# Half of the gated layers' z and u columns as seven block products, with weight sums made by accumulating DMAs

## The chip, the cores and the metric

One core of a Trainium2 chip runs the whole program: eight cores are there, seven have no part in it. The metric is the device time of one execution in microseconds, the median over the runs. The profile comes from one execution of its own.

## The reference, cut to what matters

Four residual layers work on x, 256 tokens of 1024 channels; their mixers are A, B, C and A again. The change touches the two A layers alone:

```python
def mixer_a(h, w_in, v_gain, w_s, b_s, w_out):
    proj = h @ w_in
    u = proj[..., :A_WIDTH]
    v = rms_norm(proj[..., A_WIDTH:2 * A_WIDTH], v_gain)
    z = proj[..., 2 * A_WIDTH:]
    ...
    mixed = jnp.einsum('gij,bcjgd->bcigd', ws, v) + b_s.T[None, None, :, :, None]
    ...
    y = u * mixed * jax.nn.silu(z)
    return y @ w_out
```

h is the normed x, 256 x 1024, and A_WIDTH is 2048, so u, v and z have four blocks of 512 columns each. The output is wanted in float32.

## The kernel before, in words

**Arithmetic.** Each float32 product is made as three matmuls of rounded parts (`mm3`, line 75): high by high, high by low and low by high. ACT makes a high part with a copy (`hi_of`, line 81, rows L82), DVE the low part with a subtraction (`lo_of`, line 84, rows L85).

**Weights.** The host cuts all weights into 272 units of 128 partitions x 1024 floats, 512 KB each, in the order of their use. A unit holds two k-tiles of 512 columns. SyncE loads a unit into one of four raw buffers `wr` (line 131), and ACT and DVE split it into one of seven pairs of buffers `w..h` and `w..l` (lines 142 to 152). The matmuls of a projection take the units in order (`next_unit`, line 156). After each k-tile `step` (line 163) first lets waiting tasks go on and then splits units up to five ahead of the one in use. A raw buffer is free once its low part is made, and the next load is issued then (line 154).

**Stationary operand.** h^T stands in two tiles, hTh and hTl, its high and low parts, 8 k-tiles x 256 tokens each (lines 188 and 189). `norm_transpose` (line 216) fills them for each layer. A projection by tokens (`proj_tok`, line 253) has two accumulators in PSUM, one for each 128 tokens, and takes every unit for both: 2 k-tiles x 2 token halves x 3 parts, 12 matmuls of 128x512. A block of 512 columns is four units, 48 matmuls.

**A gated layer** (`layer_a`, line 350) makes the four blocks of v, then for n = 0 to 3 the blocks z_n and u_n. Silu of z goes into a tile `sz` (line 449). `mix_task` (line 401) makes the twelve token-mixing matmuls `mx` of the block. `y_task` (line 415) makes y = u * silu(z) * (mx + b) on DVE (lines 423 and 426), transposes it on PE (line 434) and splits it. `proj_out` (line 291) is the output product, `wo`.

**What sets the order.** There is one program order. Each engine takes its instructions in that order and starts one when what it needs is there. Tasks are generators that `tick` (line 101) advances: a task gives out a few instructions and says after how many ticks it goes on. So what stands behind what on an engine is decided by the ticks, and a waiting instruction holds up all that follows on its engine. GpSimd's queue (POOL) holds the small constant loads (lines 340 to 343 and 466 to 472), the powers in the norms, and little else.

Of the kernel before, what the change touches and what calls it, by code (L numbers as in the profile page):

```python
# [17 lines left out]
P = 128  # L18
# [24 lines left out]
LAST_LAG = 1  # L43
LAST_AHEAD = 3
WARM = 24


@with_exitstack
def hybrid_trunk_kernel(ctx, tc, x, wts, norm_gainT, a_v_gain, a_wsT, a_bsT, b_gl, b_gv, c_scaleT,
# [31 lines left out]
    def hi_of(hi, src):  # L81
        nc.scalar.activation(hi, src, AF.Copy)  # L82

    def lo_of(lo, src, hi):
        nc.vector.tensor_tensor(lo, src, hi.bitcast(F32), op=ALU.subtract)  # L85
# [37 lines left out]
    used = [0]  # L123
    loaded = [0]
    split = [0]

    def load_units(n):
        while loaded[0] < min(n, n_units):
            u = loaded[0]
            raw = wp.tile([P, 2, HALF], F32, tag="wr", name=f"wr{u}", bufs=RAW_BUFS)  # L130
            nc.sync.dma_start(raw, wts[u].rearrange("p (k n) -> p k n", n=HALF))
            raws.append(raw)
            loaded[0] += 1

    lowered = [0]

    def split_hi(n):

        while split[0] < min(n, n_units):
            u = split[0]  # L140
            load_units(u + 1)
            hi, lo = pair(wp, [P, 2, HALF], "w", f"w{u}", W_BUFS)
            hi_of(hi, raws[u])
            units.append((hi, lo))
            split[0] += 1

    def split_units(n):

        split_hi(n)
        while lowered[0] < min(n, n_units):  # L150
            u = lowered[0]
            lo_of(units[u][1], raws[u], units[u][0])
            lowered[0] += 1
            load_units(u + 1 + RAW_BUFS)

    def next_unit():

# [2 lines left out]
        split_units(u + 1)  # L160
        return units[u]

    def step(i, ahead=AHEAD):

        tick()
        if i % 2 == 0:
            split_hi(used[0] + ahead)
        else:
            split_units(used[0] + ahead)
# [24 lines left out]
    gT = cp.tile([P, DEPTH * KT + 16], F32, tag="gT", name="gT")[:, :DEPTH * KT].rearrange(  # L194
        "p (l k) -> p l k", k=KT)
    nc.scalar.dma_start(gT, norm_gainT)


# [17 lines left out]
    def norm_transpose(layer, t, xs):  # L216

        pts = []
        for n in range(2):
            pt = (trp if n else atp)(f"hp{layer}{t}{n}").rearrange("p (k c) -> p k c", c=P)  # L220
            for k in range(4):
                nc.tensor.transpose(pt[:, k], xs[:, n, k * P:(k + 1) * P], ident)  # L222
            pts.append(pt)
        sl = slice(t * P, (t + 1) * P)
        for k in range(KT):
# [18 lines left out]

    def h_t(k, t):
        sl = slice(t * P, (t + 1) * P)
        return hTh[:, k, sl], hTl[:, k, sl]

    def h_all(k):
        return hTh[:, k, :], hTl[:, k, :]  # L250


    def proj_tok(name, skew=None):

        o = [pp(f"{name}_{t}") for t in range(2)]
        if skew is not None:
            ws = [next_unit() for j in range(4)]
            for t in range(2):
                need(("h", skew, t))
                for k in range(KT):  # L260
                    w = ws[k // 2]
                    mm3(o[t], h_t(k, t), (w[0][:, k % 2], w[1][:, k % 2]), k == 0, k == KT - 1)
# [12 lines left out]
        return o  # L275
# [72 lines left out]
        return kc, wsT, bsT  # L348

    def layer_a(layer, consts, pl, mid):  # L350
        kc, wsT, bsT = consts

        def tmp(tag, name, bufs):
            return pl.tile([P, HALF], F32, tag=tag, name=name, bufs=bufs)
# [5 lines left out]
        def v_task(n, o):  # L360
            vh, vl = pair(pl, [P, 2, HALF], "v", f"v{layer}{n}", 5)
            v.append((vh, vl))
            vv = [tmp("vv", f"vv{layer}{n}{t}", 2) for t in range(2)]
            for t in range(2):
                nc.scalar.activation(junk, o[t], AF.Square, accum_out=vs[t][:, n:n + 1])  # L365
                nc.vector.tensor_tensor(vv[t], o[t], kc[:, n * HALF:(n + 1) * HALF], op=ALU.mult)  # L366
            yield 1
            for t in range(2):
                hi_of(vh[:, t], vv[t])
            yield 1  # L370
            for t in range(2):
# [24 lines left out]
            mid()  # L396
# [18 lines left out]
        def y_task(n, up, us):  # L415
# [23 lines left out]
                    yield 1  # L439
            done.add(("y", layer, n))  # L440

        for n in range(4):
            spawn(v_task(n, proj_tok(f"v{layer}{n}", skew=layer if n == 0 else None)))
        for n in range(4):
            zp = proj_tok(f"z{layer}{n}")
            us = []
            for t in range(2):
                sz = tmp("sz", f"sz{layer}{n}{t}", 4)
                nc.scalar.activation(sz, zp[t], AF.Silu)  # L449
                us.append(sz)  # L450
            spawn(mix_task(n), 4)
            spawn(y_task(n, proj_tok(f"u{layer}{n}"), us))
# [28 lines left out]
                                        cs[:, a, t:t + 1, :].to_broadcast([P, 2 * NG, ROPE]), op=ALU.mult)  # L481

    def layer_b(layer, consts, pl):
        gv, msk, rop = consts
        m0, m1 = msk[:, :NG * P], msk[:, NG * P:]
        yT = []
# [241 lines left out]


    def layer_c(layer, pl):  # L730
        csc = pl.tile([P, 32], F32, name="csc")[:, :16]
        nc.gpsimd.dma_start(csc, c_scaleT)
        rcn = pl.tile([P, 4, PAD], F32, name="rcn")
# [2 lines left out]
        def tmp(tag, name, bufs):  # L736
            return pl.tile([P, HALF], F32, tag=tag, name=name, bufs=bufs)
# [309 lines left out]
```

## Time and profile before

| | |
|---|---|
| median of 3 runs | 847.01 us (846.98 to 847.21) |
| the profiled execution's own time | 846.98 us |
| its span, first to last instruction | 845.3 us |
| granted TensorE clock | 0.999 |
| PE busy | 834.2 us, 4600 matmuls |
| DVE busy, ACT busy, POOL busy | 546.7, 488.6, 56.8 us |
| loads of weight units | 272 of 512 KB, median 4.2 us from issue to landing |
| read from HBM over the span | 147.72 MB |

PE is TensorE's matmul row and PEld its weight loads, which overlap the matmuls. The time from one matmul's start to the next is its cost on a busy PE; its own duration is longer, since matmuls are pipelined. A gap in a row stands in brackets with what ended it. "L82" is a line of the kernel before; the kernel after has its own numbers.

### The profile page before, as it was taken

To read this page: it belongs to the slowest core of one execution; us is meant where nothing else is said; L and a number is where in the kernel's file an instruction comes from. 1 tells how busy PE (TensorE), PEld (TensorE's weight loads), DVE (VectorE), ACT (ScalarE), POOL (GpSimd) and SP (SyncE) were. 2 spreads that over 40 slices of the span, in tenths; PEclk is the share of its full clock that TensorE was granted. 3 is DMA by queue.
4 is the path that set the end of the run, shared out by engine and by line. 5 is a ranking of instruction groups with operands and counts; after the bars stand their busy time and mean duration, and the time that the engine had idled before them with its cause. 6 is when DMAs were issued, how large, how long until landed. Compare 5 with 4: busy or idle time off the path is not lost.

```text
span 845.3 us, 12424 instructions
## 1 busy us (share of the span) xinstructions
PE 834.2 (99%) x4600; PEld 719.2 (85%) x4600; DVE 546.7 (65%) x932; ACT 488.6 (58%) x918; POOL 56.8 (7%) x79
## 2 busy tenths in 40 slices
PE   8999999999999999999999999999999999999998
PEld 6888888888988888888888889999988888888886
DVE  6866556546747667667667576798754786556551
ACT  7665444336768677678678567446543666434340
POOL 1301000001001021021021011000000000000000
PEclk9999999999999999999999999999999999999999
DMA  8756554562755345345345267547664476455541
GB/s 297 268 207 218 197 199 155 180 193 93 253 173 157 119 150 175 124 151 174 125 150 172 79 220 255 176 150 243 203 206 149 140 235 213 158 176 172 174 149 50
DMA packets 41500, 149.57 MB, mean 177 GB/s; under 512 B 4864, under 2 KB 4880, under 8 KB 41184
## 3 DMA queue, kind: packets, MB, share of 16 engines
q1 hardware_dynamic: 40320, 144.72, 51.9%
q0 software_dynamic: 976, 4.05, 1.5%
q8 instruction: 36, 0.59, 0.3%
q14 instruction: 24, 0.20, 0.1%
q10 hardware_dynamic: 144, 0.02, 0.0%
HBM read 147.72 MB, written 1.05 MB: 176 GB/s over the span
## 4 chain that ended last, share of the span: by engine, by line
PE 86%; ACT 7%; DVE 2%; issue 2%; POOL 2%; DMA 1%; SPq 0%; POOLq 0%; DVEq 0%
PE wo L77 6%; PE wo L78 6%; PE wo L79 6%; PE qk L79 4%; PE qk L77 4%; PE qk L78 4%; PE u L79 3%; PE z L79 3%; PE z L77 3%; PE u L77 3%; PE u L78 3%; PE z L78 3%; PE v L79 3%; PE v L77 3%; PE v L78 3%; ACT junk L500 2%
## 5 line engine op out<-in xcount | busy, mean ns | idle before, releaser
L505 POOL TENSOR_TENSOR qr<-qm,m 128x4 f32<-128x4 f32 x24 | 30.3, 1271 | 224.4 <-DVE qm L504 224.4
L509 ACT ACTIVATE qn<-qk,qr 128x128 f32<-128x128 f32 x96 | 27.5, 381 | 15.1 <-POOL qr L505 15.1
L500 ACT ACTIVATE junk<-qk 128x128 bf16<-128x128 f32 x96 | 26.8, 279 | 7.3 <-PE qk L79 4.6
L423 DVE TENSOR_TENSOR sz<-u,sz 128x512 f32<-128x512 f32 x16 | 11.0, 686 | 28.0 <-PE u L79 28.0
L226 ACT ACTIVATE hTh<-hp,gT 128x128 fp32r<-128x128 f32 x64 | 17.5, 382 | 16.1 <-PE hp L222 16.1
L207 POOL TENSOR_TENSOR r<-ms,m 128x1 f32<-128x1 f32 x8 | 5.4, 670 | 285.7 <-DVE ms L205 285.7
L321 DVE TENSOR_TENSOR x<-wo,x 128x512 f32<-128x512 f32 x16 | 11.0, 690 | 20.1 <-PE wo L79 20.0
L229 DVE SCALAR_TENSOR_TENSOR hTl<-hp,gT,hTh 128x128 fp32r<-128x128 f32 x64 | 17.9, 343 | 7.8 <-ACT hTh L226 7.8
L365 ACT ACTIVATE junk<-v 128x512 bf16<-128x512 f32 x16 | 9.6, 600 | 18.1 <-PE v L79 17.9
L500 ACT ACTIVATION_READ_ACCUMULATOR junk<-qk 128x1 f32 x96 | 19.1, 199 | 0.0
L366 DVE TENSOR_TENSOR vv<-v,kc 128x512 f32<-128x512 f32 x16 | 10.9, 689 | 12.7 <-ACT junk L365 12.6
L449 ACT ACTIVATE sz<-z 128x512 f32<-128x512 f32 x16 | 9.4, 597 | 15.5 <-PE z L79 14.9
L518 DVE TENSOR_TENSOR ra<-qn,kcb 128x64 f32<-128x64 f32 x48 | 10.6, 221 | 12.0 <-ACT qn L509 10.9
L530 PE MATMUL qt<-ident,qn 128*128 128x128 f32 x96 | 14.6, 274 | 3.4 <-DVE qk12l L538 0.5
L530 PEld LDWEIGHTS qt<-ident,qn 128*128 128x128 f32 x96 | 11.3, 140 | 7.3 <-issue 2.7
L200 ACT ACTIVATE junk<-x 128x512 bf16<-128x512 f32 x16 | 10.2, 639 | 10.9 <-DVE x L321 9.4
L426 DVE SCALAR_TENSOR_TENSOR yy<-mx,bs,sz 128x256 f32<-128x256 f32 x32 | 14.0, 480 | 0.6
L600 ACT ACTIVATE p<-p,rl 128x384 f32<-128x384 f32 (+1 forms) x16 | 11.5, 769 | 4.8 <-DVE rl L599 4.8
L522 DVE TENSOR_TENSOR rb<-qn,kcb 128x32 f32<-128x32 f32 x96 | 13.8, 184 | 0.0
L596 ACT ACTIVATE p<-p,nb 128x768 f32<-128x768 f32 x8 | 7.5, 938 | 7.9 <-DVE nb L595 7.9
L504 DVE TENSOR_SCALAR qm<-qs 128x4 f32<-128x4 f32 x24 | 3.3, 165 | 12.7 <-ACT junk L500 12.7
L346 POOL TENSOR_SCALAR_AFFINE_SELECT kc<-kc 128x128 f32<-128x128 f32 x16 | 9.2, 612 | 15.4 <-DMA kc<-in_a_wsT_dram 15.4
(2770 smaller groups left out, 3262.0 us busy)
## 6 DMA issues: line engine op xcount, KB each, us to landing
wr<-in_wts_dram SPq DMA_DIRECT2D x272, 512.0 KB, 4.2
kc<-in_a_v_gain_dram POOLq DMA_DIRECT2D x2, 1024.0 KB, 6.1
x<-in_x_dram SPq DMA_DIRECT2D x4, 256.0 KB, 4.9
kc<-in_a_wsT_dram POOLq DMA_DIRECT2D x2, 512.0 KB, 8.8
out_dram<-x SPq DMA_DIRECT2D x4, 256.0 KB, 2.0
kcb<-in_masks_dram POOLq DMA_DIRECT2D x1, 576.0 KB, 8.5
kcb<-in_b_gl_dram POOLq DMA_DIRECT2D x1, 192.0 KB, 6.0
kcb<-in_rope_dram POOLq DMA_DIRECT2D x1, 64.0 KB, 8.4
```

The source lines that it names most:

```text
L77: nc.tensor.matmul(out_ap, lh[0], rh[0], start=start, stop=False, skip_group_check=True)
L78: nc.tensor.matmul(out_ap, lh[0], rh[1], start=False, stop=False, skip_group_check=True)
L79: nc.tensor.matmul(out_ap, lh[1], rh[0], start=False, stop=stop, skip_group_check=True)
L226: nc.scalar.activation(hTh[:, k, sl], pts[k // 4][:, k % 4], AF.Copy, scale=gT[:, layer, k:k + 1])
L229: nc.vector.scalar_tensor_tensor(hTl[:, k, sl], pts[k // 4][:, k % 4], gT[:, layer, k:k + 1], hTh[:, k, sl].bitcast(F32), op0=ALU.mult, op ...
L426: nc.vector.scalar_tensor_tensor(y[:, sl], mxs[n][t][:, sl], bsT[:, 2 * n + gg:2 * n + gg + 1], us[t][:, sl], op0=ALU.add, op1=ALU.mult)
L500: nc.scalar.activation(junk[:, :HD], ov[t][:, h], AF.Square, accum_out=ssq[t][:, h:h + 1])
L505: nc.gpsimd.tensor_tensor(rq[t], ms, m05, op=ALU.pow)
L509: nc.scalar.activation(qn[t][:, h], ov[t][:, h], AF.Copy, scale=rq[t][:, h:h + 1])
L522: nc.vector.tensor_tensor(rb[:, hs, s0:s0 + 16], qn[t][:, hs, s1:s1 + 16], c, op=ALU.mult)
L530: nc.tensor.transpose(pts[t][:, h], qn[t][:, h], ident)
L600: nc.scalar.activation(f, f, AF.Copy, scale=rl[i][:, 0:1])
```

## The change

In each A layer the blocks n = 1 and n = 3 of z and u are made together. Write h as a 2 x 2 matrix of blocks (two halves of 128 tokens, two halves of 512 channels) and the weights of z_n and u_n, side by side, as another: rows are the two channel halves, columns are z and u. The product of two such matrices takes eight block products, two in each of the four results. The change makes it with seven, in a known scheme of sums and differences (Winograd's form of Strassen's). Each product has four k-tiles, two units and one accumulator:

- the sums of h are made once per layer, by `sums_task` on DVE and ACT, in the v phase: four tiles, split into `sm..h` and `sm..l`
- the sums of weights are made while loading. A plain DMA brings one unit and a DMA of GpSimd adds another to the tile in place (`accum_op=ALU.add`). The list `seq` has 14 entries for a pair, in place of 8 units: the first two are u + z at k, kept in two tiles `ws`; two of z; two of u; then u is added to `ws` again; two of z; two of u + u in the `wr` buffers; then z is added to `ws`
- a product is made in one of four PSUM tiles, zb, xb, yb, wb; zb takes two products and xb three. ACT copies a partial result out (q5, p1), or its negative (n2, n3), before the next product is added to the same bank
- `first_task` and `second_task` form z and u from these on DVE, with Silu on ACT, and `mix_task` and `y_task` follow as before
- h^T becomes one tile with 16 floats to spare; in the layers A it starts 16 floats (64 bytes) higher, in B and C where it stood. gT loses the 16 floats it had to spare

The core of the diff:

```diff
+SEVEN = (1, 3)
...
+    def seven(z, u):
+        return [((u, z), "new"), ((z,), None), ((u + 2,), None), ((u + 2,), "on"), ((z + 2,), None),
+                ((u + 2, u), None), ((z + 2,), "on")]
...
+    def load_units(n=0, ahead=False):
+        while loaded[0] < n_seq and (loaded[0] < n or ahead and room()):
+            i = loaded[0]
+            us, sums = seq[i]
+            if sums and sums[:-1] == "on":
+                raw = summed[sums[-1]]
+            else:
...
+                nc.sync.dma_start(raw, wts[us[0]].rearrange("p (k n) -> p k n", n=HALF))
+                us = us[1:]
+            for u in us:
+                nc.gpsimd.dma_start(raw, wts[u].rearrange("p (k n) -> p k n", n=HALF), accum_op=ALU.add)
...
-    hTh = cp.tile([P, KT, S], F32R, tag="hTh", name="hTh")
-    hTl = cp.tile([P, KT, S], F32R, tag="hTl", name="hTl")
+    hT = cp.tile([P, 2 * KT * S + 16], F32R, tag="hT", name="hT")
+    def h_parts(layer):
+        o = 16 if layer in (0, DEPTH - 1) else 0
+        return [hT[:, o + i * KT * S:o + (i + 1) * KT * S].rearrange("p (k s) -> p k s", s=S) for i in range(2)]
...
+            zb = pp(f"zb{layer}{n}")
+            product(zb, sm(S_A21_A22), True)
+            spawn(keep_task("q5", keep, zb), 1)
+            xb = pp(f"xb{layer}{n}")
+            product(xb, lambda k: h_t(k, 0), True)
+            spawn(keep_task("p1", keep, xb), 1)
+            product(zb, sm(S_A12_REST), False)
+            product(xb, sm(S_REST), False)
+            spawn(keep_task("n2", minus, xb), 1)
+            yb = pp(f"yb{layer}{n}")
+            product(yb, lambda k: h_t(4 + k, 0), True)
...
+            spawn(first_task(), 1)
+            spawn(mix_task(n), 2)
+            product(xb, sm(S_A11_A21), False)
+            spawn(keep_task("n3", minus, xb), 1)
+            wb = pp(f"wb{layer}{n}")
+            product(wb, lambda k: h_t(4 + k, 1), True)
...
         for n in range(4):
+            if n in SEVEN:
+                seven_products(n)
+                continue
             zp = proj_tok(f"z{layer}{n}")
```

The units of the first pair are 24 to 31 before, and 24 to 37 after. GpSimd's queue before, between the second layer's constants and that layer's norm:

```order
L466 DMA kcb_661<-in_b_gl_dram 128x384
L468 DMA kcb_661<-in_masks_dram 128x1152
L470 DMA kcb_661<-in_rope_dram 128x128
L472 DMA gv_665<-in_b_gv_dram 128x6
L207 TENSOR_TENSOR r10_1633<-ms10_1631,m05_83 128x1
```

And now, at the same place; each row on `in_wts_dram` adds a unit to the tile it names:

```order
L611 DMA kcb_688<-in_b_gl_dram 128x384
L613 DMA kcb_688<-in_masks_dram 128x1152
L615 DMA kcb_688<-in_rope_dram 128x128
L617 DMA gv_692<-in_b_gv_dram 128x6
L175 DMA ws24_570<-in_wts_dram 128x1024
L175 DMA ws25_573<-in_wts_dram 128x1024
L175 DMA wr34_794<-in_wts_dram 128x1024
L175 DMA wr35_818<-in_wts_dram 128x1024
L175 DMA ws24_570<-in_wts_dram 128x1024
L175 DMA ws25_573<-in_wts_dram 128x1024
```

The additions for entries 30 and 31, 34 and 35, 36 and 37 stand behind the second layer's constants, in this order. The ones of 34 and 35 wait for the plain loads of the same tiles, and those of 36 and 37 stand behind them.

ACT before, in the pair z1,u1, from the high part of unit 34 on:

```order
L82 ACTIVATE w34h_903<-wr34_830 128x1024
L82 ACTIVATE w35h_935<-wr35_849 128x1024
L82 ACTIVATE w36h_953<-wr36_867 128x1024
L82 ACTIVATE w37h_983<-wr37_891 128x1024
L82 ACTIVATE y01h_965<-yp010_992 128x4x128
```

ACT now, from the copy p1 on:

```order
L537 ACTIVATE p101_881<-xb01_838 128x512
L83 ACTIVATE w34h_889<-wr34_794 128x1024
L83 ACTIVATE w35h_901<-wr35_818 128x1024
L83 ACTIVATE w36h_913<-ws24_570 128x1024
L83 ACTIVATE w37h_924<-ws25_573 128x1024
L532 ACTIVATE n201_930<-xb01_838 128x512
L83 ACTIVATE w38h_936<-wr38_869 128x1024
```

The copy n2 of xb, new on ACT, stands behind the high parts of entries 36 and 37, which read the tiles that GpSimd's last two additions of the pair fill.

DVE now, around the start of the pair; the rows on u, sz, mx and yy are `y_task` of block 0, and stood there before too:

```order
L86 TENSOR_TENSOR w28l_785<-wr28_657,w28h_784 128x1024
L474 TENSOR_TENSOR sz000_705<-u00_0_709,sz000_705 128x512
L477 SCALAR_TENSOR_TENSOR yy000_799<-mx000_743,bs0_187,sz000_705 128x256 x2
L474 TENSOR_TENSOR sz001_707<-u00_1_710,sz001_707 128x512
L477 SCALAR_TENSOR_TENSOR yy001_803<-mx001_750,bs0_187,sz001_707 128x256 x2
L86 TENSOR_TENSOR w29l_812<-wr29_679,w29h_811 128x1024
L86 TENSOR_TENSOR w30l_825<-ws24_570,w30h_824 128x1024
```

The low part of entry 29, behind which the load of entry 35 is issued, stands behind that gating, as unit 29's did.

More of the change, by code (lines that the diff above doesn't have):

```diff
@@ L224, in norm_transpose @@
         sl = slice(t * P, (t + 1) * P)
+        hTh, hTl = h_parts(layer)
         for k in range(KT):
@@ L440, in y_task, with sums_task @@
             done.add(("y", layer, n))
+        smh, sml = pair(pl, [P, 4, 4, P], "sm", f"sm{layer}", 1)
+        def sums_task():
+            q = {}
+            for k, t in ((1, 1), (0, 1), (0, 0), (1, 0)):
+                d = q[k, t] = tmp("sz", f"sq{layer}{k}{t}", 4).rearrange("p (k c) -> p k c", c=P)
+                hh, hl = (a[:, 4 * k:4 * k + 4, t * P:(t + 1) * P].bitcast(F32) for a in hcur)
+                nc.vector.tensor_tensor(d, hh, hl, op=ALU.add)
+                yield 1
+            a11, a12, a21, a22 = q[0, 0], q[1, 0], q[0, 1], q[1, 1]
+            for i, (d, a, b, op) in enumerate(((a22, a21, a22, ALU.subtract), (a21, a11, a21, ALU.subtract),
+                                               (a11, a22, a11, ALU.subtract), (a12, a12, a11, ALU.add))):
+                nc.vector.tensor_tensor(d, a, b, op=op)
+                hi_of(smh[:, i], d)
+                yield 1
+                lo_of(sml[:, i], d, smh[:, i])
+                yield 1
+            done.add(("sums", layer))
@@ new lines, in layer_a, with seven_products, sm, product @@
+        S_A21_A22, S_A11_A21, S_REST, S_A12_REST = range(4)
+        def seven_products(n):
+            need(("sums", layer))
+            def sm(i):
+                return lambda k: (smh[:, i, k], sml[:, i, k])
+            def product(o, a, first):
+                for j in range(2):
+                    w = next_unit()
+                    for kk in range(2):
+                        k = 2 * j + kk
+                        mm3(o, a(k), (w[0][:, kk], w[1][:, kk]), first and k == 0, k == 3)
+                        step(kk, due=kk == 1)
+            def minus(o, name):
+                d = tmp("vv", name, 2)
+                nc.scalar.activation(d, o, AF.Copy, scale=-1.0)
+                return d
+            def keep(o, name):
+                d = tmp("sz", name, 4)
+                nc.scalar.activation(d, o, AF.Copy)
+                return d
+            r = {}
+            def keep_task(key, how, o):
+                r[key] = how(o, f"{key}{layer}{n}")
+                yield 1
+            zb = pp(f"zb{layer}{n}")
[9 more added lines that the diff above has]
+            product(yb, lambda k: h_t(4 + k, 0), True)
+            z0, u0 = r["p1"], r["n2"]
+            def first_task():
+                nc.vector.tensor_tensor(z0, yb, z0, op=ALU.add)
+                nc.scalar.activation(z0, z0, AF.Silu)
+                yield 1
+                nc.vector.tensor_tensor(u0, zb, u0, op=ALU.add)
+            spawn(first_task(), 1)
[4 more added lines that the diff above has]
+            product(wb, lambda k: h_t(4 + k, 1), True)
+            z1, u1 = r["n3"], r["q5"]
+            def second_task():
+                nc.vector.tensor_tensor(u1, u1, z1, op=ALU.add)
+                nc.vector.tensor_tensor(z1, wb, z1, op=ALU.subtract)
+                nc.scalar.activation(z1, z1, AF.Silu)
+                yield 1
+            spawn(second_task(), 1)
+            spawn(y_task(n, (u0, u1), (z0, z1)), 2)
```

56 lines of the change are left out of this document (41 added, 15 removed).

## The prediction

> **What bounds the kernel now.** I read the page first: who is busy, and the chain that ended last.
>
> ```profile
> PE 834.2 (99%) x4600; PEld 719.2 (85%) x4600; DVE 546.7 (65%) x932; ACT 488.6 (58%) x918; POOL 56.8 (7%) x79
> PE 86%; ACT 7%; DVE 2%; issue 2%; POOL 2%; DMA 1%; SPq 0%; POOLq 0%; DVEq 0%
> ```
>
> PE is the bound, and the chain is 86% PE. So a matmul that disappears is worth its spacing on PE, as long as nothing new makes PE wait. Then I asked for the windows of the first gated layer, up to and through the columns z1,u1, which the change rewrites first:
>
> ```profile
> 34.00:51.00 17.00, 17.00 (x76) 13.95 (x75) 13.53 (x16) 12.74 (x21) 0.00 (x0) 1.00 0.67 233
> 56.00:67.00 11.00, 11.00 (x50) 9.03 (x49) 9.70 (x14) 9.58 (x13) 1.95 (x3) 1.00 0.45 154
> 67.00:79.60 12.60, 12.60 (x62) 10.58 (x61) 5.86 (x6) 6.26 (x8) 2.03 (x4) 1.00 0.83 269
> 79.60:103.70 24.10, 24.10 (x117) 20.09 (x116) 14.75 (x21) 10.31 (x12) 0.00 (x0) 1.00 0.59 195
> ```
>
> The columns are the stretch and then PE, PEld, DVE, ACT and POOL busy, the granted clock, the DMA share and GB/s. PE is busy in every microsecond of all four stretches, at clock 1.00. From 79.6 to 103.7 (the pair z1,u1) DVE works 14.75 of 24.1 us and ACT 10.31: there is room, but not for a doubling.
>
> **The change part by part.** The time is made against the profiled execution, 846.98 us with a span of 845.3; the median of the three runs is 847.01, so the two are the same. Below, a "unit" is one 512 KB weight tile, split by ACT into a high part and by DVE into a low part.
>
> *Fewer matmuls.* The spacing of 128x512 matmuls comes from starts in PE's timeline, 48 matmuls apart: first z0, then a stretch of wo.
>
> ```profile
> 56.20 0.39 PE L77 MATMUL z<-w16h,hTh 128*128 128x512 f32 x1
> 67.19 0.39 PE L77 MATMUL u<-w20h,hTh 128*128 128x512 f32 x1
> 805.65 0.39 PE L77 MATMUL wo<-w259h,y30h 128*128 128x512 f32 x1
> 816.53 0.39 PE L77 MATMUL wo<-w263h,y31h 128*128 128x512 f32 x1
> ```
>
> z takes (67.19 - 56.20)/48 = 0.2290 us a matmul, wo (816.53 - 805.65)/48 = 0.2267. A pair z,u has 96 matmuls now and 84 afterwards (7 products of 4 k-tiles and 3 parts). Four pairs lose 48: 48 x 0.2290 = **-11.0 us**.
>
> *h^T 64 bytes higher.* z and wo differ in the stationary operand. hTh begins, after tiles of 128-byte multiples and the 1088 bytes of junk, 64 bytes past a multiple of 128; y begins on a multiple. After the change h^T of the gated layers does too, and so do the new sums. If that is what makes wo faster, the 768 matmuls left in v, z and u and the 336 of the products gain 0.0023 us each: 1104 x 0.0023 = **-2.5 us**. It may also be nothing (0 is the other end, for the two differ in buffers as well). I take the full 2.5, as the wo rows are the only ones with such an operand at this shape.
>
> *Sums of h.* Twelve DVE operations of 128x512 in the v phase, about 0.69 us each (the rows below), are 8.3 us. In the three windows above from 34 to 51 and 56 to 79.6 DVE stands idle 3.5 + 1.3 + 6.7 = 11.5 us, and a unit is split some five units ahead of its use. I cost it at nothing. If that cover were gone, 34 to 51 alone would be short by 8.3 - 3.5 = 4.8 us per layer.
>
> *Splits.* A pair uses 14 units in place of 8, each for half as long. DVE's timeline at the start of z1, and PE's first row there:
>
> ```profile
> 70.32 1.22 DVE L85 TENSOR_TENSOR w26l<-wr,w26h 128x1024 fp32r<-128x1024 f32 x1
> 71.46 1.22 DVE L85 TENSOR_TENSOR w27l<-wr,w27h 128x1024 fp32r<-128x1024 f32 x1
> 79.12 0.69 DVE L423 TENSOR_TENSOR sz<-u,sz 128x512 f32<-128x512 f32 x1 [0.59 <-PE u L79]
> 79.84 0.88 DVE L426 SCALAR_TENSOR_TENSOR yy<-mx,bs,sz 128x256 f32<-128x256 f32 x2
> 82.14 1.22 DVE L85 TENSOR_TENSOR w29l<-wr,w29h 128x1024 fp32r<-128x1024 f32 x1
> 83.61 0.69 DVE L85 TENSOR_TENSOR y00l<-yp,y00h 128x512 fp32r<-128x512 f32 x1 [0.26 <-ACT y00h L82]
> 79.60 0.39 PE L77 MATMUL z<-w24h,hTh 128*128 128x512 f32 x1
> 82.35 0.60 PE L434 MATMUL yp<-ident,yy 128*128 128x128 f32 x4
> 82.70 0.47 PE L77 MATMUL z<-w25h,hTh 128*128 128x512 f32 x1
> ```
>
> A low part starts 1.14 us after the one ahead of it, the gating of y takes 82.14 - 79.12 = 3.0, a copy or an add 0.7. DVE's work in a new pair is 14 x 1.14 + 4 x 0.72 + 3.0 + 2 x 0.69 = 23.2 us. PE's is 84 x 0.2267 = 19.0, plus the twelve mx (1.4) and eight transposes (2 x 0.35): 21.2. DVE is over by 2.0 us, and the lead of five units (5 x 6 x 0.2267 = 6.8 us) covers that, since an ordinary pair or wo follows. I cost it at nothing; without the lead it costs 2.0 us a pair.
>
> *The sums of weights: a new wait.* This is the term that decides. The last two weight sums of a pair are made in place, on the tile that was split six units before, and Pool's queue holds them behind two other accumulates, the second of which waits for a plain load. On ACT the copy n2 (the product of units 7 and 8 with its sign turned) stands behind the high parts of both sums. The eleventh unit writes over the bank that n2 reads. So PE waits there for: plain load, accumulate, accumulate, accumulate, high part, copy. The prices of DMAs, each from the DMA issues of a window of one or two issues:
>
> ```profile
> wr<-in_wts_dram SPq DMA_DIRECT2D x1, 512.0 KB, 3.1
> wr<-in_wts_dram SPq DMA_DIRECT2D x1, 512.0 KB, 4.8
> wr<-in_wts_dram SPq DMA_DIRECT2D x1, 512.0 KB, 5.0
> kc<-in_a_v_gain_dram POOLq DMA_DIRECT2D x1, 1024.0 KB, 5.2
> kc<-in_a_wsT_dram POOLq DMA_DIRECT2D x1, 512.0 KB, 7.2
> ```
>
> The issues behind the first three, in SyncE's rows for wr, and two high parts and a copy in ACT's timeline:
>
> ```profile
> L131 SPq DMA_DIRECT2D wr<-in_wts_dram x1: 328/328/328, 83.4 to 83.4; - x1
> L131 SPq DMA_DIRECT2D wr<-in_wts_dram x1: 328/328/328, 41.3 to 41.3; - x1
> L131 SPq DMA_DIRECT2D wr<-in_wts_dram x1: 328/328/328, 43.6 to 43.6; - x1
> 68.09 1.06 ACT L82 ACTIVATE w25h<-wr 128x1024 fp32r<-128x1024 f32 x1
> 69.04 1.06 ACT L82 ACTIVATE w26h<-wr 128x1024 fp32r<-128x1024 f32 x1
> 82.98 0.60 ACT L82 ACTIVATE y00h<-yp 128x512 fp32r<-128x512 f32 x1 [4.37 <-PE yp L434]
> ```
>
> A lone 512 KB load lands 3.1 us after its issue. The loads issued at 41.3 and 43.6, with one between them, land at 46.1 and 48.6: 1.25 us of transfer each once they queue. The 1 MB load of Pool took 5.2, which is 2.7 plus two transfers.
>
> With T as the start of a pair (79.60): the low part that frees the buffer ends at 83.36, T + 3.8, and its load is issued there, landing at T + 6.9. Pool's overhead of 2.7 and three transfers of 1.25 put the last sum at T + 13.4. A high part (0.95) and the copy (0.60) end at T + 14.9. PE reaches the eleventh unit at 10 x 6 x 0.2267 + 2 x 0.35 = T + 14.3. So the wait is 0.6 us if these DMAs have the engines to themselves. SyncE issues more loads meanwhile: one, for the first unit after the pair, goes out before the last accumulate, and two more behind it. With one ahead of the last sum the wait is 0.6 + 1.25 = 1.9; with all three, 4.4. An accumulate stands in no row. Its lower end is a transfer at the plain price with nobody beside it (0.6 a pair; a gain is excluded, for nothing that exists is removed). Its upper end here is twice the plain price, as in a rival below. I take the plain price and one load ahead, the order of issue, since the nearest row, Pool's own 1 MB load, was a plain transfer: 4 x 1.9 = **+7.6 us**.
>
> Pool's loads for the next layer stand ahead of the first pair's sums, and the 7.2 above, against 2.7 + 1.25 = 3.9, shows what a transfer behind another of Pool can take. The load at 83.4, back at 3.1, shows the engines free again by then, so I add nothing; 7.2 - 3.9 = 3.3 us, once, is in the range.
>
> Sum: 846.98 - 11.0 - 2.5 + 7.6 = **841.1 us**.
>
> **The rivals.** *The sums cost double (slower).* A sum has to read the tile it adds to, so its transfer may take 2.5 us in place of 1.25. The place is the same, the three accumulates ahead of n2: T + 6.9 + 2.7 + 7.5 + 1.25 + 1.55 = T + 19.9 against T + 14.3, a wait of 5.6 us. Four pairs cost 22.4: 846.98 - 13.5 + 22.4 = 855.9 us. It decides against the change once a wait passes 13.5/4 = 3.4 us, that is once an accumulate takes 1.25 + (3.4 - 1.9)/3 = 1.75 us. For it: both operands have to pass the DMA engines. Against: in the windows the engines are 45 to 83% busy, and no row shows that a read beside a write slows them. The Trainium skill, page "DMA: Bandwidth & Descriptors", section "Rules for kernel authors", says that an accumulate "reads its destination and writes it later", and its section "SDMA does more than copy" calls the operation an elementwise reduce of two streams; no run here shows it. By a page's reading of two streams per sum the time would be the rival's.
>
> *No wait.* Were Pool's share of the engines larger or the transfers closer together, the sums would land in time: 846.98 - 13.5 = 833.5 us. For it: the shortfall at the lower end is 0.6 us of 14.3. Against: every pair has SyncE's loads beside it.
>
> *DVE becomes the bound.* If the lead is used up, each pair lasts as long as DVE's 23.2 us and not 21.2, in place of the DMA wait: 846.98 - 13.5 + 4 x 2.0 = 841.5, about the forecast. The waits would then name low parts and not DMAs. That the change does not do what it says can be left out: the order has 48 matmuls fewer.
>
> **How the numbers follow.** A measurement of this kernel tells about 0.2% (1.7 us) from no change. My forecast, a wait of 0.6 to 3.0 us a pair or DVE's 2.0, has 0.46; no wait at all 0.11; a wait of 3.0 to 3.8 a pair, which gives the gain back, 0.12; sums so slow that the time rises, 0.31. Faster is 0.46 + 0.11 = 0.57, same 0.12, slower 0.31. The range goes from the rival without a wait, 833.5, to just past the double price, 857.0; sums dearer than that, and gains beyond the first rival, are left out with less than 2 in 10. The forecast's own range is 836 (0.6 a pair) to 845.
>
> **What would show it.** PE's spacing in z0 of the first layer at 0.2267 shows the second term right, 0.229 wrong. PE's waits should list the new product on xb, released by ACT's copy n2, four times at about 1.9 us; if they are 5 us, the sums cost double, and the DMA rows of the sums will show more than 2.5 us between landings. If PE waits for low parts, the rival on DVE holds. The forecast is wrong if PE's idle time in the gated layers is below 2 us or above 13.

## The result, and the profile after

The changed kernel takes **891.95 us** (median of 4 runs, 891.0 to 892.11); the kernel before, on the same chip, 847.11 (846.98 to 847.28). The ratio is 1.0526, with an interval of 1.0513 to 1.054: slower by 44.8 us, where the prediction had 5.9 us faster, and 35 us above the end of its range. Two single executions of versions below, of 1397.9 us (shift and sums of h) and 1699.8 us (128 transposes), ran in a much slower state and are in no median here; with them these two medians would read 845.4 and 893.5 in place of 845.3 and 893.1. The profiled execution took 892.11 us, with a span of 890.4 and a mean TensorE clock of 0.972.

The page of after, its busy times and the chain that ended last, by engine and by line:

```profile
PE 830.1 (93%) x4552; PEld 714.4 (80%) x4552; DVE 596.5 (67%) x996; ACT 523.9 (59%) x966; POOL 84.4 (9%) x111
...
PE 64%; DMA 13%; ACT 8%; DVE 8%; issue 4%; POOL 2%; SPq 0%; POOLq 0%; DVEq 0%; ACTq 0%
DMA ws<-in_wts_dram 11%; PE wo L80 6%; PE wo L78 6%; PE wo L79 6%; PE qk L80 4%; PE qk L78 4%; PE qk L79 4%; PE v L79 3%; PE v L80 3%; PE v L78 3%; ACT junk L646 2%; DMA wr<-in_wts_dram 2%; PE cz L80 2%; PE cz L78 2%; PE cz L79 2%
```

PE fell from 99% busy to 93%, and transfers have gone from 1% of the chain to 13%: 11% are those into the `ws` tiles. The longest of PE's waits in after (us in total, times, longest):

```profile
PE xb L78 <- ACT n L532: 46.2, 4, 11.8
```

That is the very place which the prediction named, the eleventh unit behind the copy n2, and four times. Only the size is another: 11.5 us each, and not 1.9. PE around the first of them, with the last matmul ahead of it:

```profile
95.29 0.39 PE L80 MATMUL yb<-w33h,hT 128*128 128x512 f32 x1
107.16 0.79 PE L78 MATMUL xb<-w34h,sm0h 128*128 128x512 f32 x1 [11.48 <-ACT n L532]
107.75 0.63 PE L79 MATMUL xb<-w34l,sm0h 128*128 128x512 f32 x1
108.17 0.63 PE L80 MATMUL xb<-w34h,sm0l 128*128 128x512 f32 x1
...
110.59 0.39 PE L80 MATMUL xb<-w35h,sm0l 128*128 128x512 f32 x1
110.83 0.40 PE L78 MATMUL xb<-w35h,sm0h 128*128 128x512 f32 x1
```

Behind the wait the matmuls start 0.43 us apart at first, and only from 110.6 on 0.23 again (the granted clock was 0.50 from 107 to 110 us). What ACT did in that time shows the chain: each high part starts as its sum lands, and n2 (here `n`) comes last.

```profile
92.93 1.06 ACT L83 ACTIVATE w34h<-wr 128x1024 fp32r<-128x1024 f32 x1 [3.38 <-DMA wr<-in_wts_dram]
98.44 1.06 ACT L83 ACTIVATE w35h<-wr 128x1024 fp32r<-128x1024 f32 x1 [4.45 <-DMA wr<-in_wts_dram]
102.22 1.06 ACT L83 ACTIVATE w36h<-ws 128x1024 fp32r<-128x1024 f32 x1 [2.72 <-DMA ws<-in_wts_dram]
105.56 1.06 ACT L83 ACTIVATE w37h<-ws 128x1024 fp32r<-128x1024 f32 x1 [2.29 <-DMA ws<-in_wts_dram]
106.52 0.58 ACT L532 ACTIVATE n<-xb 128x512 f32<-128x512 f32 x1
```

The four sums land 5.5, 3.8 and 3.3 us apart. Forecast were three transfers of 1.25 us and one of SyncE's loads. SyncE's rows while the sums ran, from GpSimd's first issue at 87.5 to the last landing at 105.5:

```profile
L172 SPq DMA_DIRECT2D wr<-in_wts_dram x4: 327/328/328, 89.1 to 100.8; - x4
```

Four loads of the same size were issued while the sums ran. The first, at 89.1, went out ahead of the last sum, as forecast. The three behind it did not wait for that sum: the one issued at 95.3 took 8.3 us and landed at 103.6, ahead of it. GpSimd's queue on the two pages, before and after, gives the price of a sum in time of the 16 engines (packets, MB, share):

```profile
q0 software_dynamic: 976, 4.05, 1.5%
```

```profile
q0 software_dynamic: 5584, 20.83, 11.5%
```

Before: 1.5% of 845.3 us is 12.7. After: 11.5% of 890.4 is 102.4. The 32 sums took 89.7 us, 2.8 us each.

The first stretch, z0 of the first layer, moved as forecast. Its first matmul and the first of u:

```profile
56.20 0.39 PE L78 MATMUL z<-w16h,hT 128*128 128x512 f32 x1
67.08 0.39 PE L78 MATMUL u<-w20h,hT 128*128 128x512 f32 x1
```

(67.08 - 56.20)/48 is 0.2267 us, against 0.2290 before.

### The profile page after: what moved, and what is told of

It is laid out like the page before. It is cut to its first block, busy times and chain, and to the rows that moved or that the text cites. A ratio compares the mean times of both kernels' runs of the same rounds, so it can differ in the third digit from the quotient of the medians.

```text
span 890.4 us, 12577 instructions
## 1 busy us (share of the span) xinstructions
PE 830.1 (93%) x4552; PEld 714.4 (80%) x4552; DVE 596.5 (67%) x996; ACT 523.9 (59%) x966; POOL 84.4 (9%) x111
## 3 DMA queue, kind: packets, MB, share of 16 engines
q0 software_dynamic: 5584, 20.83, 11.5%
## 4 chain that ended last, share of the span: by engine, by line
PE 64%; DMA 13%; ACT 8%; DVE 8%; issue 4%; POOL 2%; SPq 0%; POOLq 0%; DVEq 0%; ACTq 0%
DMA ws<-in_wts_dram 11%; PE wo L80 6%; PE wo L78 6%; PE wo L79 6%; PE qk L80 4%; PE qk L78 4%; PE qk L79 4%; PE v L79 3%; PE v L80 3%; PE v L78 3%; ACT junk L646 2%; DMA wr<-in_wts_dram 2%; PE cz L80 2%; PE cz L78 2%; PE cz L79 2%
## 5 line engine op out<-in xcount | busy, mean ns | idle before, releaser
L175 POOL DMA_DIRECT2D ws<-in_wts_dram x24 | 22.1, 1020 | 178.0 <-DVE vme L434 47.0
L275 ACT ACTIVATE hT<-hp,gT 128x128 fp32r<-128x128 f32 x64 | 17.5, 383 | 16.1 <-PE hp L270 16.1
L278 DVE SCALAR_TENSOR_TENSOR hT<-hp,gT,hT 128x128 fp32r<-128x128 f32 x64 | 18.0, 343 | 7.7 <-ACT hT L275 7.7
L746 ACT ACTIVATE p<-p,rl 128x384 f32<-128x384 f32 (+1 forms) x16 | 11.5, 769 | 5.0 <-DVE rl L745 5.0
L78 PE MATMUL xb<-w34h,sm0h 128*128 128x512 f32 x2 | 1.4, 710 | 11.5 <-ACT n L532 11.5
```

Of the source, the lines that this page charges most:

```text
L78: nc.tensor.matmul(out_ap, lh[0], rh[0], start=start, stop=False, skip_group_check=True)
L175: nc.gpsimd.dma_start(raw, wts[u].rearrange("p (k n) -> p k n", n=HALF), accum_op=ALU.add)
L746: nc.scalar.activation(f, f, AF.Copy, scale=rl[i][:, 0:1])
```

## The experiments

Two theories stood against each other at first. **Price**: the addition itself makes a DMA dear. **Place**: DMAs are slow at this place, on GpSimd's queue and beside SyncE's loads, whatever they do. A third was that n2's place on ACT alone made the wait. All times below are medians; before took 846.9 to 847.2 beside them.

### Copies in place of sums

```diff
-                nc.gpsimd.dma_start(raw, wts[u].rearrange("p (k n) -> p k n", n=HALF), accum_op=ALU.add)
+                nc.gpsimd.dma_start(raw, wts[u].rearrange("p (k n) -> p k n", n=HALF))
```

> The 32 accumulating DMAs become plain copies of the same 512 KB from the same queue to the same tiles, behind the same waits; the sums of weights are left out (a copy overwrites what it should add to). Theory 'price': the addition itself makes a queued DMA take some 3.3 us in place of 1.25, so the waits of 11.6 us shrink to about 2 and the time is 841 us (835 to 847). Rival 'place': these DMAs are slow because of where they stand, on GpSimd's queue behind one another and beside SyncE's loads; then copies are as slow and the time stays between 875 and 892.

Measured: 865.8 us, ratio 1.0213 (1.0188 to 1.0239). It fits neither. PE's longest wait, and GpSimd's queue on the page:

```profile
PE xb L78 <- ACT n L532: 23.9, 4, 7.0
```

```profile
q0 software_dynamic: 5584, 20.83, 6.9%
```

A copy takes (6.9% x 865.6 - 12.7)/32 = 1.5 us of the engines against 2.8 for a sum, so the addition has a price, and 26.2 us go with it. But the waits are still 6.0 us each, and the forecast of 1.9 had been worked out at just this plain price. The price explains a good half of the 44.8 us, no more.

### The copy n2 earlier

```diff
-            product(xb, sm(S_REST), False)
-            spawn(keep_task("n2", minus, xb), 1)
+            product(xb, sm(S_REST), False, keep_task("n2", minus, xb))
```

The task is started ahead of the last `step` of the product.

> The copy n2 is given to ACT ahead of the high parts of entries 36 and 37, the rest as it is. Rival 'order on ACT': the wait was made by n2's place alone, and the time falls below 847. Theory 'price': the first wait ends when the high part of entry 35 is done (at T + 20.0, 7 us sooner), but the last two sums still land at T + 22.7 and T + 26.0, and the product wb needs them; a pair ends about 6 us sooner, 4 x 6 = 24, and the time is about 868 us (860 to 875).

Measured: 885.9 us, ratio 1.0456 (1.0442 to 1.047), above the theory's 860 to 875 and far from the rival's 847. n2 had come ahead of one high part only, that of entry 37. The next run splits entry 36 one unit later too (`AHEAD - 1` in that product), so that n2 stands ahead of both.

> As the run before with n2 ahead, which put it ahead of entry 37's high part alone (ACT's rows show 36's still in front); here it stands ahead of both. Theory 'price and traffic': PE's wait at the eleventh unit falls from 8.8 to about 4.6 us, but wb waits for the last two sums, which land at T + 22 and T + 25; a pair takes 30 to 31 us against 33.0, and the time is 875 to 880 us. Rival 'order on ACT': below 850.

Measured: 886.2 us, ratio 1.0457 (1.0438 to 1.0475), again above the forecast, 875 to 880. The first pair's n2 now starts at 100.12, right behind the high part of entry 35:

```profile
99.16 1.06 ACT L83 ACTIVATE w35h<-wr 128x1024 fp32r<-128x1024 f32 x1 [2.47 <-DMA wr<-in_wts_dram]
100.12 0.58 ACT L534 ACTIVATE n<-xb 128x512 f32<-128x512 f32 x1
101.60 1.06 ACT L83 ACTIVATE w36h<-ws 128x1024 fp32r<-128x1024 f32 x1 [0.90 <-DMA ws<-in_wts_dram]
```

The wait there fell to 5.9 us, and the time did not follow. The windows of this kernel, the first pair and then the block z2 (columns as in the prediction):

```profile
79.30:110.55 31.25, 23.77 (x106) 18.70 (x105) 18.45 (x25) 12.81 (x16) 3.44 (x4) 0.89 0.81 222
110.55:126.30 15.75, 12.79 (x57) 9.66 (x58) 14.02 (x18) 8.51 (x11) 1.70 (x2) 1.00 0.79 265
```

and the same two in the changed kernel:

```profile
79.40:115.70 36.30, 23.65 (x106) 18.87 (x104) 23.80 (x30) 17.32 (x21) 3.45 (x4) 0.86 0.79 219
115.70:127.50 11.80, 11.80 (x57) 9.79 (x56) 9.46 (x14) 4.68 (x6) 1.70 (x2) 1.00 0.95 307
```

The pair takes 5.0 us less (31.25 against 36.3), and z2 takes 4.0 more: DVE is busy 14.0 of its 15.75 us with what the late sums had held up, and PE waits for DVE there. So n2's place on ACT is worth some 6 of the 45 us and not more: what hangs on the late sums only waits elsewhere.

### SyncE's loads behind the sums

```diff
+    on = [i for i in range(n_seq) if (seq[i][1] or "")[:-1] == "on"]
+    late = {i + k for i in on[3::4] for k in range(1, 5)}
...
-                nc.sync.dma_start(raw, wts[us[0]].rearrange("p (k n) -> p k n", n=HALF))
+                (nc.gpsimd if i in late else nc.sync).dma_start(raw, wts[us[0]].rearrange("p (k n) -> p k n", n=HALF))
```

> The four plain loads that follow a pair's last sum (entries 38 to 41 after the first pair) are issued from GpSimd's queue, so that they stand behind the sums and take no part of the DMA engines while these run. Theory 'traffic': between the sums stand three of SyncE's loads of 1.58 us each; without them the sums land 2.8 us apart in place of 5.5, 3.8 and 3.3, n2 comes 3 to 4.5 us sooner in each pair, and the time is 874 to 880 us. Rival 'the sum itself': a sum needs its 3.3 us or more alone, and the time stays at 892 (889 to 895).

Measured: 875.1 us, ratio 1.0328 (1.0312 to 1.0344), inside the theory's 874 to 880. ACT in the first pair:

```profile
93.12 1.06 ACT L83 ACTIVATE w34h<-wr 128x1024 fp32r<-128x1024 f32 x1 [4.21 <-DMA wr<-in_wts_dram]
95.68 1.06 ACT L83 ACTIVATE w35h<-wr 128x1024 fp32r<-128x1024 f32 x1 [1.50 <-DMA wr<-in_wts_dram]
98.17 1.06 ACT L83 ACTIVATE w36h<-ws 128x1024 fp32r<-128x1024 f32 x1 [1.44 <-DMA ws<-in_wts_dram]
100.68 1.06 ACT L83 ACTIVATE w37h<-ws 128x1024 fp32r<-128x1024 f32 x1 [1.45 <-DMA ws<-in_wts_dram]
```

With nobody between them (SyncE's queue moves nothing from 89 to 103 us) the sums land 2.5 us apart, and n2 ends 4.9 us sooner (at 102.2, where the changed kernel has 107.1). So 2.5 us is what a sum costs; 3.3 to 5.5 is what it costs beside SyncE's loads. The Trainium skill, page "DMA: Bandwidth & Descriptors", section "Queues, rings and completion order", says that each engine goes round robin between the queues that have work for it, packet by packet. The traces agree: in the changed kernel, ahead of the second sum's landing (95.2 to 98.4 us), the sums' queue took 68.0% of the engines' time and SyncE's 37.3% (by their packets, which overlap a little), so a load of SyncE beside the sums does not stand ahead of them or behind them, it takes its share from each.

### Both at once

> Both at once: the additions are plain copies (sums of weights left out) and the four loads after a pair stand behind them on GpSimd's queue. The prediction's wait of 1.9 us a pair assumed the plain price of 1.25 us and one of SyncE's loads between. Theory 'two causes': the price of a sum and SyncE's loads beside it are all that was mis-sized; with both taken away the copies land 1.3 us apart, the wait is 0.6 to 2.5 us, and the time is 836 to 845 us. Rival 'a third cause' (the copies land no sooner because GpSimd's issues or the load ahead of them are late): 850 us or more.

Measured: 847.4 us (845.07 to 853.2, 10 runs), ratio 1.0011 (0.999 to 1.0032). The profiled execution took 845.55. Its waits, and ACT in the first pair, which starts at 78.58 here:

```profile
PE xb L78 <- ACT n L534: 8.2, 4, 3.1
```

```profile
91.39 1.06 ACT L83 ACTIVATE w35h<-wr 128x1024 fp32r<-128x1024 f32 x1 [2.20 <-DMA wr<-in_wts_dram]
92.67 1.06 ACT L83 ACTIVATE w36h<-ws 128x1024 fp32r<-128x1024 f32 x1 [0.22 <-DMA ws<-in_wts_dram]
93.97 1.06 ACT L83 ACTIVATE w37h<-ws 128x1024 fp32r<-128x1024 f32 x1 [0.24 <-DMA ws<-in_wts_dram]
94.93 0.58 ACT L534 ACTIVATE n<-xb 128x512 f32<-128x512 f32 x1
```

The copies land 1.3 us apart, and the wait is 2.05 us a pair on the average, 1.3 to 3.1 in the four: this is the chain that the prediction had drawn up, and its 1.9 us. The time lies 2.4 us beyond the theory's range, short of the rival's; the profiled execution is 8.2 us of waits and 3.2 more above the kernel without additions, below. Of the 3.2, 1.5 are a lower TensorE clock (shown below) behind the longest of the waits, 3.1 us in the last pair: the twelve matmuls there take 3.97 us from first to last, where eleven steps of 0.2267 are 2.49. The rest is open. These runs scatter more than others, and the scatter goes with the clock: the five at 845.1 to 846.0 us have a mean clock of 0.997 or 0.998, the five at 848.8 to 853.2 of 0.991 to 0.995, as longer waits would give; that the waits differ is not shown. The four kernels make a square:

| | SyncE's loads beside | loads behind |
|---|---|---|
| sums | 892.0 | 875.1 |
| plain copies | 865.8 | 847.4 |

The price is worth 26.2 and 27.7 us, the loads 16.9 and 18.4. The two add up, to within 1.5 us, and together they make 44.6 us.

### No additions

The inner loop over the further units is left out, and with it the additions' DMAs.

> The 32 additions are left out altogether, with their DMAs (the sums hold one addend only); products, splits, copies and gating stay. Theory: with no chain of sums the waits at the eleventh unit go, and the prediction's rival without a wait holds: 833.5 us (831 to 837). Rival 'DVE': the splits of 14 units and the gating, 23.2 us of DVE a pair against 21.2 on TensorE, make a wait of their own; then PE waits for low parts and the time is about 841 us.

Measured: 834.1 us, ratio 0.9848 (0.9835 to 0.9861). The window of the first pair:

```profile
78.60:100.10 21.50, 21.50 (x106) 18.01 (x105) 21.32 (x28) 16.29 (x20) 0.00 (x0) 1.00 0.53 176
```

PE is busy throughout. DVE works 21.32 of 21.5 us, and no low part makes PE wait: the lead covers it, but nothing is left over.

### A sum by itself

Behind the end of the changed kernel four plain copies, eight sums and four loads were added.

> The changed kernel with 16 DMAs of 512 KB behind its end, to four buffers: four plain copies on GpSimd's queue, four sums and four more on it, four plain loads on SyncE's. By the queues' packets a sum takes 2.78 us of all 16 engines and a plain one 1.5: alone they land 2.8 and 1.5 us apart. Rival 'place': with nobody beside, a sum lands as fast as a plain copy. Rival 'latency': sums land over 3.3 us apart even here.

One execution: 908.6 us. GpSimd's issues of the second four sums, each of which waits for the landing of one of the first four:

```profile
879.90 0.85 POOL L1061 DMA_DIRECT2D alone<-in_wts_dram  x1 [3.79 <-DMA alone<-in_wts_dram]
882.38 0.84 POOL L1061 DMA_DIRECT2D alone<-in_wts_dram  x1 [1.64 <-DMA alone<-in_wts_dram]
885.15 0.84 POOL L1061 DMA_DIRECT2D alone<-in_wts_dram  x1 [1.92 <-DMA alone<-in_wts_dram]
888.95 0.85 POOL L1061 DMA_DIRECT2D alone<-in_wts_dram  x1 [2.95 <-DMA alone<-in_wts_dram]
```

Sums land 2.5 and 2.8 us apart, with none of the kernel's loads beside them: the price is the sum's own, and the rival 'place' fails. The last step, 3.8, has the output's transfers beside it. The plain copies waited for their buffers and did not queue, so they give no spacing here.

### The clock in the wait

```diff
+            wb = pp(f"wb{layer}{n}")
+            for _ in range(96):
+                nc.tensor.transpose(wb[:, :P], ident, ident)
             product(xb, sm(S_A11_A21), False)
```

> 96 transposes of the identity, 10.5 us of work, are put on TensorE between the product yb and the third product of xb, where it waits. Theory: the matmuls after a wait come 0.427 us apart (8 to 12 of them, 8.6 us in the four pairs together) because TensorE stood idle; kept busy it goes on at 0.227, and the time is 892 - 8.6 = 883 us (881 to 886). Rival: the slow matmuls have another cause, such as operands that come late; then the time is 892 or more, and the spacing stays 0.427.

Measured: 893.1 us, ratio 1.0543 (1.0528 to 1.0557): no gain. The transposes ended too early. In three pairs 2.56, 2.15 and 2.44 us of waiting were left, and the matmuls were slow again; rows of the second of these pairs, and then of the one pair with less waiting, where all spacings were short:

```profile
168.82 0.50 PE L78 MATMUL xb<-w56h,sm0h 128*128 128x512 f32 x1 [2.15 <-ACT n L532]
...
170.05 0.63 PE L79 MATMUL xb<-w56l,sm0h 128*128 128x512 f32 x1
170.48 0.63 PE L80 MATMUL xb<-w56h,sm0l 128*128 128x512 f32 x1
```

```profile
774.67 0.50 PE L78 MATMUL xb<-w254h,sm3h 128*128 128x512 f32 x1 [1.46 <-ACT n L532]
775.01 0.39 PE L79 MATMUL xb<-w254l,sm3h 128*128 128x512 f32 x1
775.24 0.40 PE L80 MATMUL xb<-w254h,sm3l 128*128 128x512 f32 x1
...
777.30 0.39 PE L80 MATMUL xb<-w255h,sm3l 128*128 128x512 f32 x1
```

> 128 transposes in place of 96 in the wait. With 96 they ended 1.7 to 2.8 us ahead of n2, and the matmuls were slow again from about 1.4 us after the start of xb on, but not in the one pair where 1.7 us were left. If idle time lowers the clock, all twelve matmuls of xb now come 0.227 us apart in all pairs, and the time is 884 to 889 us; if the clock follows something else, some stay at 0.427 and the time is 892 or more.

Measured: 893.1 us, ratio 1.0543 (1.0524 to 1.0561). The same kernel once more, profiled:

> The kernel with 128 transposes in the wait once more, for a profile. It took 893.5 us at a clock of 1.00, so the slow matmuls were not worth their 8.6 us. Theory 'backlog': DVE, which is busy 17.2 of the 18 us behind the first wait of the changed kernel, sets the end of that stretch; the twelve matmuls of xb come 0.227 us apart here, and TensorE waits for DVE or ACT behind them instead. Rival: the transposes last beyond n2 and take away what the clock gives; then xb starts more than 1.5 us behind the end of n2.

One execution: 894.5 us at a clock of 1.00, and no spacing of 0.43 is left in any pair. So idle time lowers the clock. The Trainium skill, page "TensorE: Matmul & The Clock Gate", section "Part 1: The HAM clock gate", has the array at half clock after an idle window of some 3.4 us; the traces agree for the long waits (0.43 us behind 11.5 us of waiting) and the shortest (0.23 behind 1.46), but here the clock also fell behind waits shorter than 3.4 us, down to 2.15.

What the half clock costs in time stays open. In the changed kernel the twelve matmuls behind the four waits are 8.0 us slower from first to last (4.13, 4.86, 4.12 and 4.86 us in place of 2.49; the 8.6 of the expectation was a rougher count). With the clock kept, the transposes went on past the end of n2 by 0.7 to 1.3 us, 4.5 in all, and n2 itself ended 1.0 to 2.7 us later in its pair; for the latter I have no cause. The twelve matmuls gained 7.6 us here (2.6 in each pair), the transposes took 4.5 and n2's delays add up to 6.3: together 3.2 us more, and the profiled execution took 2.4 more than that of the changed kernel. So the half clock is worth about 8 us if nothing else moves (an estimate from these rows); no run shows that as a gain. The theory of a backlog is not shown: it forecast waits of PE behind xb, and no row has one, though DVE is busy nearly all of 107 to 125 in the changed kernel:

```profile
107.00:125.00 18.00, 17.84 (x81) 14.89 (x82) 17.25 (x24) 10.05 (x14) 1.70 (x2) 0.91 0.69 229
```

### The shift of h^T and the sums of h

`SEVEN = ()` leaves all pairs as before, with h^T 64 bytes higher and the sums of h made but not used:

> No pair is made by seven products (all four blocks as before), but h^T stands 64 bytes higher and the sums of h are made and not used. By the prediction's second and third terms: 1152 matmuls x 0.0023 = 2.6 us less than before, the sums of h at nothing: 844.4 us (843.5 to 845.5). Rival: the start of h^T does not matter, 847.0. Rival: the sums of h are not hidden, up to 4.8 us a layer more.

Measured: 845.3 us, ratio 0.9978 (0.9969 to 0.9987). Then the shift alone:

> The kernel before with h^T 64 bytes higher and nothing else: no seven products, no sums of h. With the unused sums it took 845.4, 1.9 us below before. If the sums of h cost nothing, the same 845.4 (844.9 to 845.9); if they cost what was missing to the predicted 2.6 us, 844.4.

Measured: 845.4 us, ratio 0.9978 (0.9969 to 0.9988). The sums of h cost nothing that these runs can tell, and the shift gives 1.8 us, short of the 2.6. Of the versions that compute everything, these two are the only ones below both kernels.

### Other ways to make the sums

GpSimd's own additions in place of DMAs; `wr` units are loaded, u a second time, and added with `nc.gpsimd.tensor_tensor`:

> The weight sums are made by GpSimd from loaded units, eight additions of 128x1024 a pair, in place of accumulating DMAs; a pair loads ten units, all on SyncE's queue. No run shows such an addition yet. If one takes 2 us, a pair needs 16 us of GpSimd beside 21.2 of TensorE, the sums are in time and the time is 834 to 842 us, below both kernels. Rival: one takes 3 us or more, or slows DVE's splits beside it; then the wait for the last two sums stays in part and the time is above 847.

Measured: 865.1 us, ratio 1.0215 (1.0201 to 1.0229). The time is the rival's, by its second reason: the splits beside an addition are slowed. GpSimd's additions on `ws` over the run, and DVE in the first pair:

```profile
L151 POOL TENSOR_TENSOR ws<-ws,wr 128x1024 f32<-128x1024 f32 x24 | 69.5, 2895 | 132.1 <-DMA wr<-in_wts_dram 98.4 <-DVE y01l L86 21.1 <-issue 5.6
```

```profile
87.13 3.36 DVE L86 TENSOR_TENSOR w30l<-ws,w30h 128x1024 fp32r<-128x1024 f32 x1
...
93.75 3.40 DVE L86 TENSOR_TENSOR w32l<-wr,w32h 128x1024 fp32r<-128x1024 f32 x1
```

An addition takes 2.9 us, and a low part beside it up to 3.4 in place of 1.22. The Trainium skill, page "SBUF — State Buffer", section "SBUF: two separate sides", says that a DVE operation with two SBUF inputs and a GpSimd operation that reads SBUF hold one pair of ports in turn, each for the whole instruction; the rows agree. The wait for the last two sums, which the rival had kept in part, is in no row: the longest waits are those of the transposes of y for DVE, up to 3.8 us.

DVE's own additions for the two sums on `ws`, with wb ahead of the third product of xb:

```diff
+            for i in (u, u + 1):
+                if i in adds:
+                    nc.vector.tensor_tensor(raws[i], raws[i], adds.pop(i), op=ALU.add)
             hi_of(hi, raws[u])
```

> A version meant to keep the seven products and shorten the chain: the two sums on the ws tiles are made by DVE from units that stand in SBUF anyway (four subtraction-sized operations of 1.14 us a pair), only u + z and the other u + u stay with accumulating DMAs, and the product wb comes ahead of the third product of xb. A pair then has 10 plain loads and 4 sums, 10 x 1.27 + 4 x 2.5 = 22.7 us of the DMA engines in place of 32.7. Theory 'chain': the wait, now for two sums in a row and not four, is 0 to 3 us a pair, and the time is 834 to 846 us, below both kernels. Rival 'DVE': with 27.8 us a pair against 21.2 on TensorE DVE becomes the bound, and the time is 850 to 860 us.

Measured: 858.7 us, ratio 1.0133 (1.0115 to 1.0151), inside the rival's 850 to 860. The waits are no longer on n2; the longest are on the transposes of y, which wait for DVE. The two longest, and the window of the first pair:

```profile
PE yp L496 <- DVE y32l L86: 3.5, 1, 3.5
PE yp L496 <- DVE y02l L86: 3.3, 1, 3.3
```

```profile
79.40:105.30 25.90, 23.28 (x105) 19.20 (x105) 24.68 (x31) 14.70 (x18) 1.75 (x2) 0.93 0.74 217
```

DVE is busy 24.7 of the 25.9 us of the first pair. In these three ways nobody had the time to spare for the sums: not the DMA engines, not GpSimd beside DVE, not DVE.

## Why the prediction was wrong

- **Bound and place: right.** PE was the bound, and the new wait stands where it was put, at the eleventh unit, on n2, four times. By the prediction's own sign (PE idle for more than 13 us there) the forecast was wrong: it was 46.2.
- **Fewer matmuls, splits, sums of h: right.** Without additions the time was 834.1, and the rival without a wait had 833.5. The splits cost nothing there, and the sums of h nothing (845.3 with, 845.4 without). The cover of the splits was thin: DVE worked 21.32 of the pair's 21.5 us.
- **h^T: right in kind, a little too large.** 1.8 us for 1152 matmuls, where 0.0023 us each had given 2.6. z0's spacing is the forecast one, 0.2267; on the average over all blocks the gain was 1.8/1152 = 0.0016.
- **The wait: the step that failed**, in its words "I take the plain price and one load ahead, the order of issue". Both halves were too low. A sum costs 2.5 us and not 1.25. And the order of issue is no order of service between two queues: SyncE's loads, four of them and not one, shared the engines with the sums throughout. Taking each away alone was worth 26 or 17 us, both together 44.6, and then the wait was the predicted one, 2.05 against 1.9 us. That the place of the wait and this remainder came out is the mechanism being right and not luck; the two sizes were taken at or near the low end of what the prediction itself had listed (1.25 to 2.5 us a sum; no load, one or three).
- **The rival of the double price was right in its price** (2.5 us, as measured) **and far off in its time** (855.9 against 892.0). It had the same one load ahead; but with the loads behind the sums the time was still 875.1, with waits of 7.2 us a pair against its 5.6, so that is not the whole of its miss. The reason given against it, that no row shows a read beside a write to be slow, had no row on either side and should have carried no weight.
- **The first pair, step by step.** The load of entry 35 was to be issued at T + 3.8 and to land at T + 6.9, with T = 79.42 here. It was issued at 85.06 by the trace, T + 5.6, and took 4.1 us (first row below), T + 9.7. The 1.8 us of delay come from the pair's own first sums, which the prediction had not put on this path: ACT waited 4.1 us for the sum of entry 24 (its high part starts at 71.8), and DVE came late to the gating and to the low part of entry 29 behind it. From there to the last sum 7.7 us had been allowed (2.7, three transfers and one load); it took 105.5 - 89.2 = 16.3. With both causes taken away (T = 78.58) the load was issued at 82.37, T + 3.8, and took 3.1 us (second row), T + 6.9; n2 ended at 95.5, T + 16.9, where T + 14.9 and 1.25 for the load had been forecast, T + 16.2.

```profile
wr<-in_wts_dram SPq DMA_DIRECT2D x1, 512.0 KB, 4.1
```

```profile
wr<-in_wts_dram SPq DMA_DIRECT2D x1, 512.0 KB, 3.1
```

- **What was not in the sum at all**: the engines' total. A pair brings ten plain loads of 1.5 us and eight sums of 2.8, 37 us of the DMA engines for 21 us of TensorE's work. Even at the plain price 18 transfers of 1.25 are 22.5 us (an estimate), more than those 21, which would have warned of any chain that waits its turn. The half clock behind a long wait was not in it either.

Of the 45 us the runs have shown the two causes, and that they add up. Against the forecast the miss is 50.9 us (891.95 - 841.1): 44.6 are the two causes, and of the 6.3 that are left 0.6 are the wait and 0.8 h^T; the rest is open but for the half clock named above. Against the kernel without additions the changed one takes 57.8 us more; 46.2 are the waits on n2, and some 8 the half clock behind them. How much DVE's backlog adds is not shown.

## What to carry to other kernels

When transfers are added, add up the engines' time per stage first, at the dearest price that isn't excluded, and only then follow the chain. Between two queues these transfers were not served in the order of issue: count every load that is issued before the last of the chain lands. And where an unseen operation decides the sign, do not let the nearest row of another operation price it: here a sum took twice a copy.

## What was not expected of the hardware

- An accumulating DMA of 512 KB takes about 2.5 us behind another one and 2.8 us of the engines' time, a plain one 1.3 and 1.5. Its issue takes GpSimd 0.85 us.
- An addition of 128x1024 float32 on GpSimd takes 2.9 us and stretches DVE's subtractions beside it from 1.22 to as much as 3.4 us.
- A start 64 bytes higher of the stationary operand changes the matmul spacing in z0 from 0.2290 to 0.2267 us, and the time by 1.8 us (ratio 0.9978).
- The clock fell to half behind waits of 2.15 to 2.56 us (96 transposes), but not behind one of 2.25 (plain copies, loads behind): here the length of the wait alone did not decide.
